# Two rows per block: summing the two partial results of an outer product before they are weighed, instead of weighing each

## The chip, the cores and the metric

The kernel runs on one core of a Trainium2 chip. A core has five engines that run their own queues in order: TensorE (PE, matrix multiplication into the accumulator memory PSUM), VectorE (DVE), ScalarE (ACT), GpSimd (POOL) and SyncE (SP), which here only issues transfers (DMA) between the main memory and the on-chip memory SBUF. PSUM has eight banks of 128 x 512 fp32 values. The metric is the time of one execution on the device in microseconds (us), given as the median of several runs.

## The reference

One layer of an encoder over a sequence of 2048 with 1024 features: an attention part and then a two-layer perceptron, each with a normalization ahead of it and a gate behind it. The change lies in the last line, in the second multiplication:

```
x = x + gt1 * (mixed @ w_o[l])
h = rmsnorm(x, g_norm2[l]) * (1.0 + sc2) + sh2
x = x + gt2 * (jnp.square(jax.nn.relu(h @ w1[l])) @ w2[l])
```

`w1` is 1024 x 4096 and `w2` is 4096 x 1024. The kernel holds everything transposed: features are rows, positions are columns. `gt2` is one factor per feature, so one per row.

## The kernel before, in words

**Seven products instead of eight, twice.** Both multiplications of the perceptron are done blockwise with the scheme that needs seven products of half-size blocks in place of eight (numbered 1 to 7 here); sums and differences of blocks are made ahead on VectorE. In the second multiplication, five of the seven products (`DOUBLE = (7, 2, 5, 3, 4)`, in this order) are cut once more in the same way. So each of these five is a stage of its own, made by the function `outer` and the class `Outer`, with seven inner products in the order `OUTER = (1, 5, 6, 3, 7, 2, 4)`. Here "stage 7" is the outer product 7, and "inner product 7" one of the seven in a stage. Products 1 and 6 (`PLAIN`) aren't cut again; product 1 runs ahead of stage 7, product 6 between stage 7 and stage 2.

**A step.** An inner product has eight steps (`HP`), a stage 56. A step does six matmuls: for each of two 128-row halves `n` of the result three, because every operand is held as a rounded high part and a remainder, and high x high, high x remainder and remainder x high are added up in PSUM (`mm3`). The high part is made by ScalarE (a cast), the remainder by VectorE (a subtraction); both go to one of eight operand buffers (pool `opp`, tile names `opr` for the moving operand, `ol` for two steps' worth of the fixed one). The planning loop at the end of the kernel prepares operands ahead of the step that multiplies as long as no more than eight of these buffers are taken. A step takes one and a half of them on average.

**Banks.** Inner products share accumulators (`HOME`): 1 and 2 add up in one pair of banks, 5 and 3 in a second, 6, 7 and 4 in a third, which starts as ScalarE's copy of the result of inner product 1. Four blocks of the result come out of this: block "12" is the second pair as it stands after inner product 3, plus the third pair as it stands after inner product 6. Block "22" is the second pair as it stands after inner product 5, plus the third pair as it stands after 7. Block "11" is the first pair after 2, block "21" the third pair after 4.

**Where a block goes.** A block of an outer product enters one block of rows of the output or two. Stages 2, 3 and 4 have one, stages 7 and 5 two ("two rows per block"). In `end`, called after the last step of an inner product for each half `n`, VectorE does for each target row tile `x`: x = (bank * gate) + x. This is `weigh`, one instruction on 128 x 512 values (SCALAR_TENSOR_TENSOR in the profile). The blocks "22" and "12" arrive in two parts, so their tiles are weighed into twice, once after each part: in stages 7 and 5 there are four weighings (two halves, two rows) after each of the inner products 5, 6, 3, 7, 2 and 4. After the last part of a block the tile is stored, by a transfer queued on SyncE two steps later (`later.add(2, ...)`): back to the scratch `scr_x`, or, where this was the row's last contribution, to the output.

**Rows.** The tiles `x` are loaded from `scr_x` by `load_x`, four per block in stages 7 and 5. Its step is counted from the start of the stage: block "22" at step 9, "12" at 11, "11" at 35, "21" at 43. Tiles come from two pools: `temp` (seven buffers; names in the profile begin with t, as `txo`) and `kept` (twelve buffers, names with c, as `cxo`). Four of the kept buffers hold the result of product 1 (`cs`) until stage 2 has used it.

**Order.** The queues of TensorE and SyncE follow the order of the program strictly. On VectorE and ScalarE instructions stand in the order in which the planning loop emits them: at each step first the preparation of operands ahead, then the jobs set for this step by `at` (among them the differences of operand tiles on 128 x 1024 values, `r<-r,r` in the profile, and the issue of loads), then the step's matmuls and what `end` adds, then the delayed stores.

In the profile all instructions have the line 42, that of a helper, so that tiles are told apart by name: `ps` and `ps_s` are accumulators (`ps_s` the pair that starts as a copy), `l` and `r` raw operands, `ol` and `opr` the prepared ones, `mod` holds the gates.

Of the kernel before, what the change touches and what calls it, by code (L numbers as in the profile page):

```python
# [13 lines left out]
ALU = mybir.AluOpType  # L14
# [65 lines left out]
def encoder_kernel(ctx, tc, xT, c, g1, g2, w_in, w_rest, gqk, bias, w_o, w1, w2, w_ada, b_ada, out):  # L80
    nc = tc.nc
    act, dve, pool, sp = nc.scalar, nc.vector, nc.gpsimd, nc.sync
# [161 lines left out]
    if True:  # L244
# [208 lines left out]
        def load_x(tb, q=None):  # L453
            xts[tb] = []
            for k in range(KT):
                xt = xp.tile([P, TB], F32, tag="xt", name=f"xt{tb}_{k}")
                (q or sp).dma_start(xt, xT[k * P : (k + 1) * P, tb * TB : (tb + 1) * TB])
                xts[tb].append(xt)
# [34 lines left out]
        act, dve, pool = (Ordered(tc, e) for e in (act, dve, pool))  # L493
# [7 lines left out]
        keep_busy(36, idle)  # L501
        act.activation(cg[:, 0:1], zero, AF.Sigmoid)
        load_x(3, osp)
        osp.dma_start(cb, c.partition_broadcast(P))
        osp.dma_start(bcol, b_ada)
# [64 lines left out]
        for k in range(KT):  # L570
# [18 lines left out]
            if k == KT - 3:  # L589
                load_raw(*loads.pop(0), osp)  # L590
                load_x(2, osp)
# [91 lines left out]
    if True:  # L683
# [68 lines left out]
        class Unit:  # L752


            def __init__(self, h, g, first, last):
                self.h, self.g, self.first, self.last = h, g, first, last
                self.nm = f"{self.ca}_{h}_{g}"
                self.ws = []
                self.wt = {}
# [19 lines left out]
            def values(self, j):  # L779
                if j == 0 and self.first:  # L780
                    pend["acc"] = ppo.tile([P, TB], F32, tag="acc", name=f"acc{self.nm}")
                self.acc = pend["acc"]
                wh, wl, cols, kb = self.wt.pop(j)
                end = self.last and j == len(self.blocks) - 1
                pe.matmul(self.acc[:, cols], self.v[:, kb, :], wh[:, cols], start=self.first and j == 0, stop=False)
                pe.matmul(self.acc[:, cols], self.v[:, kb, :], wl[:, cols], start=False, stop=end)
                if end:
                    soon.append(lambda: finish(self))
# [487 lines left out]
        for i in range(len(steps) + LAG):  # L1276
# [8 lines left out]
            done = list(soon)  # L1285
# [40 lines left out]
    PLAIN = (1, 6)  # L1326
    DOUBLE = (7, 2, 5, 3, 4)
    OUTER = (1, 5, 6, 3, 7, 2, 4)
    OUTER_NAME = {1: "11", 2: "12", 4: "22"}
    HOME = {1: 1, 2: 1, 5: 5, 3: 5, 6: 6, 7: 6, 4: 6}  # L1330
    HP = NP // 2
# [6 lines left out]
    if True:  # L1338
# [9 lines left out]
        def operand(src, nm, eng=None, dst=None):  # L1348

            o = opp.tile([P, 2, TB], F32R, tag="op", name=f"op{nm}") if dst is None else dst  # L1350
            split(o[:, 0, :], o[:, 1, :], src, eng)
            return o
# [8 lines left out]
        def column_sum(eng, out, a, b, op):  # L1361
            eng.tensor_tensor(out, a, b, op=op)
            return out
# [4 lines left out]
        def kept(nm):  # L1368
            return accp.tile([P, TB], F32, tag="c", name=f"c{nm}")

        def bank(nm, banks=pp):
            return banks.tile([P, TB], F32, tag="ps", name=f"ps{nm}")
# [3 lines left out]
        def at(n, job):  # L1376
            jobs.setdefault(n, []).append(job)
# [108 lines left out]
        class Step:  # L1486
            tiles = frees = 1

            def ready(self):
                return True  # L1490
# [7 lines left out]
        class First(Step):  # L1498
# [4 lines left out]
            def __init__(self, mb, j, i):  # L1503
                self.mb, self.j, self.i, self.nm = mb, j, i, f"{mb}_{j}_{i}"
                if mb and j == 0 and i in OUTER[:2]:
                    self.tiles = self.frees = 0

            def ready(self):
                return OUTER_NAME.get(self.i, self.i) in First.pair.get((self.mb, self.j), ())

            def prepare(self, home=None):
                if (home is None) != (self.tiles > 0):
                    return
                d, i = First.pair[self.mb, self.j], self.i
                self.w = operand(d[OUTER_NAME.get(i, i)], f"w{self.nm}", dst=home)

# [24 lines left out]
            def run(self):  # L1541
# [34 lines left out]
                if i == 4:  # L1576
                    c21 = self.hidden(kept(f"z{nm}"), 2, ps)

                    def end():
                        self.keep(4, column_sum(dve, kept(f"e{nm}"), c21, d["t2"], ALU.subtract))  # L1580
                        del First.pair[self.mb, self.j]

                    later.add(3, end)
# [98 lines left out]
        def weigh(x, a, n):  # L1682
            dve.scalar_tensor_tensor(x, a, mod[:, 5 * KT + n : 5 * KT + n + 1], x, op0=ALU.mult, op1=ALU.add)

        def rows_of(t, mb, n, odd):
            tb = 2 * mb + odd
            return t[n * P : (n + 1) * P, tb * TB : (tb + 1) * TB]
# [26 lines left out]
        def plain(mb, i):  # L1714

            f = len(steps)
            steps.extend(Second(mb, i, j) for j in range(NP))
            if i == 6:
                for n, step in enumerate((4, 5, 6, 12)):
                    update(mb, n, f + step, temp, False)  # L1720
            return f
# [48 lines left out]
        class Outer(Step):  # L1770
# [4 lines left out]
            def __init__(self, i, q, k):  # L1775
                self.i, self.q, self.pr, self.k = i, q, OUTER[q], k
                self.nm = f"{i}_{self.pr}_{k}"
# [43 lines left out]
            def end(self, n):  # L1821
                pr, ps = self.pr, Outer.banks[HOME[self.pr], n]
                if pr == 1:
                    Outer.banks[6, n] = bank(f"{self.nm}_s{n}", seeded)
                    act.copy(Outer.banks[6, n], ps)
                for b, done in {5: (("22", 0),), 6: (("12", 0),), 3: (("12", 1),), 7: (("22", 1),), 2: (("11", 1),), 4: (("21", 1),)}.get(pr, ()):
                    for x, mb, row, odd, last in Outer.outs[b, n]:
                        weigh(x, ps, row)
                        if done:
                            dst = rows_of(out, mb, row, odd) if last else scr_x[2 * mb + odd, row]  # L1830
                            later.add(2, lambda dst=dst, x=x: sp.dma_start(dst, x))

            def load_x(self, b):
                home = kept if self.i in (5, 7) and b in ("22", "11") else temp
                for n in range(2):
                    Outer.outs[b, n] = []
                    for r, odd in {2: ((0, 1),), 3: ((0, 0),), 4: ((1, 1),), 7: ((1, 1), (1, 0)), 5: ((0, 0), (1, 0))}[self.i]:
                        mb, row = 2 - int(b[1]), HK * r + 2 * (int(b[0]) - 1) + n
                        x = home(f"xo{self.i}_{b}_{n}{odd}")
                        sp.dma_start(x, scr_x[2 * mb + odd, row])  # L1840
                        Outer.outs[b, n].append((x, mb, row, odd, self.i in (2, 3, 4) or (self.i == 5 and r > 0)))
# [3 lines left out]
        def half(i, pr, g):  # L1845

            mb, a = {1: (1, 0), 5: (0, 0), 3: (0, 1), 2: (1, 1)}[pr]
            t = halves[pr, g] = hop[g].tile([P, 2, TB], F32, tag=f"h{pr}_{g}", name=f"r{i}_{pr}_{g}")
            sp.dma_start(t, scr_hid[mb, i, HP // 2 * a + g])

        def half_sum(i, pr, g):

            if pr == 5:
                column_sum(dve, halves[5, g], halves[5, g], halves[1, g], ALU.subtract)
                return
            x, y = {6: (3, 5), 7: (6, 1), 4: (2, 6)}[pr]
            t = hop[g].tile([P, 2, TB], F32, tag=f"h{pr}_{g}", name=f"r{i}_{pr}_{g}")
            column_sum(dve, t, halves[x, g], halves[y, g], ALU.subtract)
            halves[pr, g] = t

        def outer(i, plan):

            f = len(steps)
            steps.extend(Outer(i, q, k) for q in range(7) for k in range(HP))
            for g in range(HP // 2):
                for pr, (begin, gap) in plan["load"].items():
                    at(begin + gap * g, lambda pr=pr, g=g: half(i, pr, g))
                for pr, (begin, gap) in plan["sum"].items():
                    at(begin + gap * g, lambda pr=pr, g=g: half_sum(i, pr, g))
            for q in range(7):  # L1870
                at(f + HP * q - 12, steps[f + HP * q].load)
            for pr, b in ((5, "22"), (6, "12"), (2, "11"), (4, "21")):
                s = steps[f + HP * OUTER.index(pr)]
                at(f + HP * OUTER.index(pr) + (1 if b == "22" else -5), lambda s=s, b=b: s.load_x(b))
            return f

        class Mixed(Step):
# [45 lines left out]
        for mb in (1, 0):  # L1923
            begin = len(steps)
            steps += [First(mb, j, i) for j in range(NP) for i in OUTER]
            end = len(steps)
            for j in range(NP):
                f = steps[begin + 7 * j]
# [41 lines left out]
        f = plain(0, 1)  # L1970
# [4 lines left out]
        for i in DOUBLE:  # L1975
            f = outer(i, plan)
# [119 lines left out]
```

## Time and profile before

| | us |
|---|---|
| median of 3 runs | 2537.08 |
| lowest, highest | 2535.84, 2537.11 |
| the profiled execution | 2536.57 |
| its span, first to last instruction | 2534.8 |

The profile shows one execution. "Busy" is the time in which an engine had an instruction under way; VectorE's and ScalarE's instructions overlap their followers a little, so what an instruction costs its queue is read from start to start, not from its duration. Matmuls are pipelined: the duration of one is far longer than the distance to the next. In a list of instructions in order of time, equal neighbours are merged (x48), the first number is the start in us, and a bracket tells how long the engine was idle before and which engine's result ended it. SPq are transfers issued on SyncE's queue. The granted clock of TensorE was 0.998 over the span.

### The profile page before, as it was taken

What the parts mean: (1) busy time and instruction counts of PE and PEld (TensorE: products, weight loads), DVE (VectorE), ACT (ScalarE), POOL (GpSimd) and SP (SyncE); (2) the same over time, 40 slices, a digit from 0 to 9 for tenths busy, and PEclk for the clock granted to TensorE, in tenths of its full rate; (3) what the DMA queues carried; (4) which work ended last, traced back from release to release, by engine and by line L of the source; (5) the groups of instructions that cost most, each with busy time, mean ns of one, the idle gap of its engine ahead of it and who ended that gap; (6) DMA issues with size and microseconds to landing.
All of it is one profiled execution on the core that took longest, in us unless ns stands there. A gap on an engine that the chain in (4) does not pass through costs nothing.

```text
span 2534.8 us, 39551 instructions
## 1 busy us (share of the span) xinstructions
PE 2511.2 (99%) x12388; PEld 2097.2 (83%) x12388; DVE 2032.4 (80%) x3577; ACT 1523.8 (60%) x2917; POOL 773.9 (31%) x1160
## 2 busy tenths in 40 slices
PE   9999999999999999999999999999999999999999
PEld 8888888888878888788888888888888888888787
DVE  7656776887789988999868777779877759799998
ACT  6334424668866687666755555567555546576665
POOL 4330154776766677777620000000000000010000
PEclk9999999999999999999999999999999999999999
DMA  9879968779977788766777889996998996888882
GB/s 356 325 300 361 354 272 293 225 244 289 297 246 250 236 245 268 257 196 212 228 284 260 298 278 321 328 351 207 315 323 270 314 365 260 321 248 286 299 282 84
DMA packets 300755, 706.29 MB, mean 279 GB/s; under 512 B 32256, under 2 KB 91648, under 8 KB 288896
## 3 DMA queue, kind: packets, MB, share of 16 engines
q1 hardware_dynamic: 294640, 690.65, 79.5%
q0 software_dynamic: 4608, 8.39, 1.9%
q10 hardware_dynamic: 1296, 4.72, 0.5%
q8 instruction: 98, 1.61, 0.3%
q14 instruction: 113, 0.93, 0.1%
HBM read 476.61 MB, written 227.02 MB: 278 GB/s over the span
## 4 chain that ended last, share of the span: by engine, by line
PE 48%; DVE 7%; ACT 1%; DMA 1%; issue 1%; SPq 0%; POOL 0%; DVEq 0%; ACTq 0%; POOLq 0%
PE ps L42 25%; PE ps_s L42 14%; PE po L42 3%; PE acc L42 2%; PE wt L42 2%; DVE opr L42 2%; PE z L42 1%; DVE ol L42 1%; DVE r L42 1%; DVE h L42 1%; DVE txo L42 0%; PE cz L42 0%; ACT cy L42 0%; DVE cy L42 0%; ACT h L42 0%
## 5 line engine op out<-in xcount | busy, mean ns | idle before, releaser
L42 PE MATMUL ps<-h,opw 128*128 128x512 f32 x1512 | 358.6, 390 | 0.0
L42 ACT CAST wth<-wt 128x512 fp32r<-128x512 f32 (+3 forms) x544 | 257.1, 484 | 167.8 <-PE wt L42 157.1
L42 POOL TENSOR_TENSOR b<-p 128x512 f32<-128x512 f32 (+1 forms) x320 | 291.9, 912 | 167.1 <-DVE p L42 103.8
L42 DVE TENSOR_TENSOR wtl<-wt,wth 128x512 fp32r<-128x512 f32 (+3 forms) x544 | 291.0, 547 | 60.8 <-ACT wth L42 58.1
L42 PEld LDWEIGHTS ps<-h,opw 128*128 128x128 f32 x1512 | 283.9, 188 | 58.7
L42 PE MATMUL pt<-w,ht 128*128 128x512 f32 x1248 | 288.2, 391 | 0.0
L42 PE MATMUL ps_s<-h,opw 128*128 128x512 f32 x1152 | 277.5, 390 | 0.7 <-DVE cp L42 0.3
L42 PEld LDWEIGHTS pt<-w,ht 128*128 128x128 f32 x1248 | 233.1, 188 | 47.6
L42 DVE TENSOR_TENSOR_SCAN p<-z,p,zero 128x512 f32<-128x512 f32 x192 | 245.5, 1280 | 21.2 <-ACT z L42 16.4
L42 PEld LDWEIGHTS ps_s<-h,opw 128*128 128x128 f32 x1152 | 215.9, 188 | 46.7 <-DVE cp L42 0.9
L42 ACT CAST opr<-r 128x512 fp32r<-128x512 f32 x280 | 174.3, 623 | 129.1 <-PE ps L42 72.1
L42 PE MATMUL ps<-opr,ol 128*128 128x512 f32 x960 | 222.0, 390 | 0.4 <-DVE opr L42 0.3
L42 PE MATMUL acc<-wth,v 128*128 128x512 f32 (+3 forms) x544 | 220.9, 410 | 0.1
L42 PEld LDWEIGHTS ps<-opr,ol 128*128 128x128 f32 x960 | 179.9, 188 | 40.1 <-DVE opr L42 1.9
L42 ACT ACTIVATE z<-z 128x512 f32<-128x512 f32 (+1 forms) x320 | 166.5, 521 | 55.4 <-PE z L42 50.7
L42 DVE TENSOR_TENSOR opr<-r,opr 128x512 fp32r<-128x512 f32 x280 | 184.4, 681 | 10.8 <-ACT opr L42 10.0
L42 PE MATMUL z<-k,q 128*128 128x512 f32 (+3 forms) x640 | 185.8, 372 | 6.2 <-DVE p L42 5.5
L42 PE MATMUL acc<-wtl,v 128*128 128x512 f32 (+3 forms) x544 | 185.8, 348 | 0.1
L42 POOL DMA_DIRECT2D scr_x<-txu x12 | 10.5, 878 | 546.8 <-ACT txu L42 546.8
L42 PE MATMUL ps<-oph,opv 128*128 128x512 f32 x768 | 175.2, 390 | 0.3 <-DVE txo L42 0.2
L42 PE MATMUL wt<-ident,b 128*128 128x128 f32 x1088 | 171.2, 273 | 0.2 <-DVE p L42 0.2
L42 PEld LDWEIGHTS ps<-oph,opv 128*128 128x128 f32 x768 | 144.1, 188 | 30.9 <-DVE txo L42 0.6
(223 smaller groups left out, 5052.3 us busy)
## 6 DMA issues: line engine op xcount, KB each, us to landing
r<-scr_hid SPq DMA_DIRECT2D x80, 512.0 KB, 6.6
q<-scr_q SPq DMA_DIRECT2D x128, 256.0 KB, 5.3
w<-in_w_dram SPq DMA_DIRECT2D x64, 512.0 KB, 5.8
k<-scr_k SPq DMA_DIRECT2D x240, 128.0 KB, 4.1
v<-scr_v SPq DMA_DIRECT2D x120, 256.0 KB, 4.3
wa<-in_w_ada_dram SPq DMA_DIRECT2D x48, 512.0 KB, 6.2
ow<-scr_wo SPq DMA_DIRECT2D x24, 1024.0 KB, 6.7
l<-scr_t SPq DMA_DIRECT2D x20, 1024.0 KB, 7.7
```

The lines of the kernel that those rows point to most:

```text
L42: return lambda *x, **y: self.tc.keep_in_program_order(f(*x, **y))
```

## The change

In stages 5 and 7 the two parts of block "22" and of block "12" are no longer weighed one by one. After inner product 5 (block "22") and 6 (block "12") ScalarE copies the two banks to tiles of the kept pool. After inner product 7 (block "22") and 3 (block "12") VectorE adds the bank to this copy, and the sum is weighed into each of the two rows, once. The row tiles of "22" and "12" are therefore loaded later, five steps ahead of inner product 7 and of inner product 3 (steps 27 and 19). The row tiles of "22" and "21" come from the kept pool, those of "12" and "11" from the temporary one; before, "22" and "11" were kept. Blocks "11" and "21" are weighed as before, and the other three stages don't change.

```
+    TWICE = (5, 7)
...
                 for b, done in {5: (("22", 0),), 6: (("12", 0),), 3: (("12", 1),), 7: (("22", 1),), 2: (("11", 1),), 4: (("21", 1),)}.get(pr, ()):
+                    if self.i in TWICE and b[1] == "2":
+                        if not done:
+                            Outer.outs[b, n, "part"] = kept(f"q{self.nm}_{n}")
+                            act.copy(Outer.outs[b, n, "part"], ps)
+                            continue
+                        c = Outer.outs.pop((b, n, "part"))
+                        ps = column_sum(dve, c, ps, c, ALU.add)
                     for x, mb, row, odd, last in Outer.outs[b, n]:
                         weigh(x, ps, row)
...
             def load_x(self, b):
-                home = kept if self.i in (5, 7) and b in ("22", "11") else temp
+                home = kept if self.i in TWICE and b in ("22", "21") else temp
...
-            for pr, b in ((5, "22"), (6, "12"), (2, "11"), (4, "21")):
+            for pr, b in ((7 if i in TWICE else 5, "22"), (3 if i in TWICE else 6, "12"), (2, "11"), (4, "21")):
                 s = steps[f + HP * OUTER.index(pr)]
-                at(f + HP * OUTER.index(pr) + (1 if b == "22" else -5), lambda s=s, b=b: s.load_x(b))
+                at(f + HP * OUTER.index(pr) + (1 if pr == 5 else -5), lambda s=s, b=b: s.load_x(b))
```

## The prediction

> **What bounds the kernel now.** I read the page's first lines first, then the busy time by stretches of time, cut at the stages that the change touches.
>
> ```profile
> PE 2511.2 (99%) x12388; PEld 2097.2 (83%) x12388; DVE 2032.4 (80%) x3577; ACT 1523.8 (60%) x2917; POOL 773.9 (31%) x1160
> ```
> ```profile
> core 0: us, PE busy (x) PEld busy (x) DVE busy (x) ACT busy (x) POOL busy (x), PEclk, DMA share, GB/s
> 2101.60:2178.10 76.50, 76.50 (x338) 63.05 (x337) 74.77 (x114) 50.94 (x88) 0.00 (x0) 1.00 0.82 310
> 2298.20:2377.80 79.60, 78.43 (x337) 62.66 (x337) 79.60 (x120) 50.43 (x86) 0.00 (x0) 1.00 0.84 289
> ```
>
> TensorE bounds the whole. The two stretches are the outer stages of product 7 and product 5 of the second multiplication (stage 7, stage 5 below), the only ones that change. There VectorE is as full as TensorE: 74.77 of 76.50, and 79.60 of 79.60 us. Next, TensorE in order of time; a row starts where the accumulating bank changes, and 48 matmuls are one inner product.
>
> ```profile
> 2101.60 21.92 PE L42 MATMUL ps<-opr,ol 128*128 128x512 f32 x96
> ...
> 2156.00 11.38 PE L42 MATMUL ps<-opr,ol 128*128 128x512 f32 x48
> 2167.21 11.04 PE L42 MATMUL ps_s<-opr,ol 128*128 128x512 f32 x48
> 2178.09 1.52 PE L42 MATMUL ps<-oph,opv 128*128 128x512 f32 x6
> 2179.78 42.46 PE L42 MATMUL ps<-oph,opv 128*128 128x512 f32 x186 [0.17 <-DVE txo L42]
> ...
> 2298.24 21.92 PE L42 MATMUL ps<-opr,ol 128*128 128x512 f32 x96
> ...
> 2330.88 11.58 PE L42 MATMUL ps<-opr,ol 128*128 128x512 f32 x48
> 2342.30 5.83 PE L42 MATMUL ps_s<-opr,ol 128*128 128x512 f32 x25
> ...
> 2354.83 7.83 PE L42 MATMUL ps<-opr,ol 128*128 128x512 f32 x31
> ...
> 2366.94 11.04 PE L42 MATMUL ps_s<-opr,ol 128*128 128x512 f32 x48
> 2377.82 22.17 PE L42 MATMUL ps<-opr,ol 128*128 128x512 f32 x96
> ```
>
> An undisturbed inner product takes 10.88 us (2366.94 to 2377.82), a step (six matmuls) 1.36, a stage of seven 76.16. Stage 7 takes 2178.09 - 2101.60 = 76.49: 0.33 lost, all between 2156.00 and 2167.21, inner product 2. Stage 5 takes 79.58: 3.42 lost, of it 0.54 in inner product 3 (from 2330.88), 1.65 in 7 (from 2342.30), 1.23 in 2 (from 2354.83). So 3.75 us is nearly all that there is to win. VectorE in stage 7 says how the loss comes about; idle time before an instruction stands in brackets.
>
> ```profile
> 2132.37 0.69 DVE L42 TENSOR_TENSOR opr<-r,opr 128x512 fp32r<-128x512 f32 x1 [0.67 <-ACT opr L42]
> ...
> 2144.74 0.69 DVE L42 TENSOR_TENSOR opr<-r,opr 128x512 fp32r<-128x512 f32 x1
> 2145.34 2.72 DVE L42 SCALAR_TENSOR_TENSOR txo<-ps,mod,txo 128x512 f32<-128x512 f32 x4
> 2147.97 0.68 DVE L42 TENSOR_TENSOR opr<-r,opr 128x512 fp32r<-128x512 f32 x1
> ...
> 2157.47 2.72 DVE L42 SCALAR_TENSOR_TENSOR cxo<-ps_s,mod,cxo 128x512 f32<-128x512 f32 x4
> 2160.11 0.68 DVE L42 TENSOR_TENSOR opr<-r,opr 128x512 fp32r<-128x512 f32 x1
> ...
> 2161.31 1.22 DVE L42 TENSOR_TENSOR r<-r,r 128x1024 f32<-128x1024 f32 x1
> 2162.44 1.29 DVE L42 TENSOR_TENSOR opr<-r,opr 128x512 fp32r<-128x512 f32 x2
> ```
> ```profile
> 2143.95 0.62 ACT L42 CAST opr<-r 128x512 fp32r<-128x512 f32 x1 [0.22 <-PE ps L42]
> ```
> ```profile
> 2163.18 3.77 PEld L42 LDWEIGHTS ps<-opr,ol 128*128 128x128 f32 x17 [0.42 <-DVE opr L42]
> ```
>
> Four weighings at the end of an inner product occupy VectorE for 2.63 us (2145.34 to 2147.97), 0.66 each, and what stands behind them in its queue are remainders (opr, ol), which TensorE multiplies by. Up to 2144.74 VectorE keeps pace: at 2132.37 it stood idle for ScalarE's cast, and the cast waits for TensorE to give back an operand buffer. From 2145.34 on it never rests, is late by the end of inner product 7 (the weighings start at 2157.47, when inner product 2 has been running for 1.47), gets four more, and in inner product 2 the weight load at 2163.18 waits 0.42 for a remainder. In stage 5 the same queue was late before:
>
> ```profile
> 2320.86 2.71 DVE L42 SCALAR_TENSOR_TENSOR cxo<-ps,mod,cxo 128x512 f32<-128x512 f32 x4
> ...
> 2332.99 2.71 DVE L42 SCALAR_TENSOR_TENSOR txo<-ps_s,mod,txo 128x512 f32<-128x512 f32 x4
> ...
> 2345.12 2.71 DVE L42 SCALAR_TENSOR_TENSOR txo<-ps,mod,txo 128x512 f32<-128x512 f32 x4
> ...
> 2357.25 2.71 DVE L42 SCALAR_TENSOR_TENSOR cxo<-ps_s,mod,cxo 128x512 f32<-128x512 f32 x4
> ...
> 2362.22 1.27 DVE L42 TENSOR_TENSOR opr<-r,opr 128x512 fp32r<-128x512 f32 x2
> ```
>
> **The change part by part.** *Weighings removed.* Each stage loses four after inner product 5 and four after 6: 8 x 0.66 = 5.28 us of VectorE. *Sums added.* Two before the four weighings after 3, two before those after 7. These rows price them: a sum out of PSUM and its follower; two dependent sums; a weighing whose inputs all lie in SBUF.
>
> ```profile
> 1804.61 0.68 DVE L42 TENSOR_TENSOR cp<-ps,cp 128x512 f32<-128x512 f32 x1
> 1805.21 0.68 DVE L42 TENSOR_TENSOR opw<-w,opw 128x512 fp32r<-128x512 f32 x1
> ```
> ```profile
> 1813.08 0.68 DVE L42 TENSOR_TENSOR ca<-cp,cy 128x512 f32<-128x512 f32 x1
> 1813.80 0.69 DVE L42 TENSOR_TENSOR cb<-cp,ca 128x512 f32<-128x512 f32 x1
> ```
> ```profile
> 21.24 0.74 DVE L42 SCALAR_TENSOR_TENSOR ht<-xt,mod,ht 128x512 fp32r<-128x512 f32 x1
> 21.90 1.27 DVE L42 CUSTOM_DVE_ANT_0 wa<-wa,cs,bcol 128x1024 f32<-128x1024 f32 x1
> ```
>
> A sum holds the queue for 0.60 (1804.61 to 1805.21) if its follower doesn't need it, for 0.72 (1813.08 to 1813.80) if it does. The weighing behind each sum reads it, so I take s = 0.72. A weighing from SBUF takes 0.66 (21.24 to 21.90), as from PSUM: no change. The Trainium skill, "Perfetto Trace Analysis", section "Optimizing Scalar/DVE Operations", gives VectorE some 125 ns of access overhead on PSUM against 60 on SBUF; by it each of the 16 weighings would get about 0.065 us cheaper (an estimate from that page), 1.0 us off the result below. The two 0.66 steps of the rows don't bear it out, and I leave it out of the sum.
>
> *Stage 7.* The 5.28 us come off where VectorE had time: it can't run ahead, because its work waits for casts and those for buffers. What remains of the relief is that the remainder at 2144.74 can start when its cast (2143.95 + 0.62 = 2144.57) is done: 0.17 sooner. From there to the wait at 2163.18 VectorE has no gap, so every added us is a us for TensorE: 4 x 0.72 = 2.88. Loss afterwards 0.33 - 0.17 + 2.88 = 3.04 instead of 0.33: **+2.71**.
>
> *Stage 5.* Without the eight weighings the queue would reach the end of inner product 3 at 2345.12 - 5.28 = 2339.84, before TensorE (2330.88 + 10.88 = 2341.76): it has caught up, and stands as stage 7 does at that place. What follows has the same length in both: 12.13 us from the weighings after 3 to those after 7 (2145.34 to 2157.47; 2345.12 to 2357.25), 4.97 on to the remainders that TensorE waits for (2162.44; 2362.22). So it loses 3.04 too, instead of 3.42: **-0.38**.
>
> *ScalarE's copies,* four a stage:
>
> ```profile
> L42 ACT COPY cp<-ps 128x512 f32<-128x512 f32 x32 | 18.8, 588 | 32.2 <-PE ps L42 32.2
> L42 ACT CAST opr<-r 128x512 fp32r<-128x512 f32 x280 | 174.3, 623 | 129.1 <-PE ps L42 72.1 <-PE ps_s L42 47.5 <-DVE opr L42 8.1
> ```
>
> Two are 1.18 us after inner product 5 and again after 6, with a wait for the last matmuls; the casts behind them wait for those matmuls' buffers anyway, and have 129.1 / 280 = 0.46 us of slack each, so ScalarE is level again after three casts. The cover is the operand lead of eight buffers, 1.5 a step: five steps, 6.8 us. I cost them at nothing; without that cover it would be 1.18 for each pair. The banks copied are written again one inner product (10.88) later: no wait.
>
> *Loads of rows moved.* Sixteen a stage as before. "22" goes from step 9 to 27, "12" from 11 to 19, and they pass loads of operands on SyncE's queue.
>
> ```profile
> 2150.89 2.52 SPq L42 DMA_DIRECT2D l<-scr_s  x4
> ```
> ```profile
> DMA to landing us min/median/max: 4.9/6.4/11.4
> ```
>
> "12" has 12 steps, 16.3 us, before it is read. The tightest operand is that of inner product 4, whose issue (2150.89 to 2153.41) stands behind the stores of "12" and the loads of "11", which now take a fourth temporary that these stores set free. It moves by the two sums, 1.44, and with the longest landing of this tile, 11.4, arrives at 2166.3; cast and remainder (0.62 + 0.68) make 2167.6, and TensorE wants it at 2167.21 + 2.71 = 2169.92. Cost: nothing; beyond a landing of 13.7 us, one us for each us. The parts and "22" fill the twelve kept buffers of stage 7 together with the four sums of the plain stage; "21" takes the parts' buffers, which come free with the weighings that the stores ahead of it on SyncE's queue wait for anyway: nothing. No instruction is moved past another on GpSimd's queue. The 0.17 at 2179.78 stays: the wait in inner product 2 leaves VectorE just ahead of TensorE in both kernels.
>
> **Sum:** 2.71 - 0.38 = 2.33, in general 8s - 3.43. Profiled execution 2536.57 + 2.3 = 2538.9; it lies 0.51 below the median 2537.08, so 2539.4 as a median, slower by 0.09%.
>
> **Rivals.** *A, the relief carries over.* VectorE has 16 x 0.66 = 10.56 us of this work in a stage now, 4 x 0.72 + 8 x 0.66 = 8.16 then. If the 2.4 us counted as a total, both losses would vanish: -3.75, 2533.3. For it: 79.60 busy of 79.60 in stage 5. Against: the idle time at 2132.37 and the cast at 2143.95, which show that it can't work ahead of the second half. The same section of the Trainium skill's page would have work moved to ScalarE where VectorE is saturated; whether that holds where the work kept is bunched is what A decides.
>
> *B, the hand-over inside the sums is dearer (slower).* A weighing that waits for a sum out of PSUM is a pair that this trace doesn't have. The price is 8 us per us of s. It passes 0.2% (5.07 us) at s = 1.06; at 1.13, what the 128x1024 sums take (2161.31 to 2162.44), it gives 5.61 and 2542.7.
>
> *C, the operand of inner product 4 comes late* because of the moved loads: beyond the 13.7 us above. If it were 2.8 us later than that in one stage, 2542.2. Against: the longest landing of all is 11.4.
>
> **How the numbers follow.** 0.2% is about what a measurement of this kernel can tell from no change. My forecast: 0.64; s from 0.60 (independent) to 0.86 (0.74, the longest row, and 0.12 of hand-over) gives 1.37 to 3.45, its own range 2538.5 to 2540.5. A: 0.16, of it 0.06 for a gain of over 0.2%, more than the losses in these rows hold. B: 0.14. C and other delays: 0.06. Faster 0.06, same 0.64 + 0.10 = 0.74, slower 0.20. Cases of both signs are open, so the range runs from A's 2533.3 to B's 2542.7.
>
> **What would show it.** VectorE: four sums and eight weighings a stage with a copied part as input, sum to weighing 0.72. TensorE: stage 7 near 79.2 us, the lost time in inner products 7 and 2, its wait on a remainder; stage 5 near 79.2 with nothing lost in inner product 3. ScalarE: four copies a stage of 0.59. Wrong if stage 7 stays at 76.5 (A), if sum to weighing takes over 1 us (B), or if ScalarE waits for that operand's load (C).

## The result, and the profile after

| | before | after |
|---|---|---|
| median, lowest to highest of 19 runs each, us | 2536.73 (2535.25 to 2538.56) | 2540.56 (2538.40 to 2545.38) |
| the profiled execution, its span, us | 2536.57, 2534.8 | 2540.6, 2538.9 |
| stage 7: length less the undisturbed 76.16 | 0.33 | 4.19 |
| stage 5: the same | 3.42 | 4.49 |

The change makes the kernel slower, by a ratio of 1.0016 (95% interval 1.0010 to 1.0022). A second series with the same kernel, called "again" below, gave 2539.80 beside 2536.43, 1.0013 (1.0004 to 1.0022). The first line of the page, busy time by engine:

```profile
PE 2511.6 (99%) x12388; PEld 2096.6 (83%) x12388; DVE 2028.8 (80%) x3569; ACT 1527.8 (60%) x2925; POOL 773.9 (30%) x1160
```

VectorE is busy for 3.6 us less than before (2032.4), and the profiled execution takes 4 us more. TensorE of the kernel after, in order of time, stage 7 and then stage 5, the seven inner products in the order 1, 5, 6, 3, 7, 2, 4:

```profile
2101.10 21.92 PE L42 MATMUL ps<-opr,ol 128*128 128x512 f32 x96
...
2144.61 7.19 PE L42 MATMUL ps_s<-opr,ol 128*128 128x512 f32 x31
2151.96 4.15 PE L42 MATMUL ps_s<-opr,ol 128*128 128x512 f32 x17 [0.16 <-DVE opr L42]
2155.95 5.83 PE L42 MATMUL ps<-opr,ol 128*128 128x512 f32 x25
2163.22 7.50 PE L42 MATMUL ps<-opr,ol 128*128 128x512 f32 x23 [1.45 <-DVE opr L42]
2170.56 11.04 PE L42 MATMUL ps_s<-opr,ol 128*128 128x512 f32 x48
2181.44 4.82 PE L42 MATMUL ps<-oph,opv 128*128 128x512 f32 x19
...
2301.47 21.92 PE L42 MATMUL ps<-opr,ol 128*128 128x512 f32 x96
...
2344.99 7.19 PE L42 MATMUL ps_s<-opr,ol 128*128 128x512 f32 x31
...
2356.36 5.83 PE L42 MATMUL ps<-opr,ol 128*128 128x512 f32 x25
2363.61 2.16 PE L42 MATMUL ps<-opr,ol 128*128 128x512 f32 x6 [1.43 <-DVE opr L42]
...
2371.24 11.04 PE L42 MATMUL ps_s<-opr,ol 128*128 128x512 f32 x48
2382.12 4.24 PE L42 MATMUL ps<-opr,ol 128*128 128x512 f32 x18
```

From row to row, less 10.88 each: stage 7 loses 0.46 in inner product 7 (2144.61 to 2155.95) and 3.73 in 2 (2155.95 to 2170.56). Stage 5 loses 0.49 in 7 (2344.99 to 2356.36) and 4.00 in 2, and nothing ahead of that (2344.99 - 2301.47 is four times 10.88); inner product 3, which lost 0.54 before, is clean. Both waits are for a remainder from VectorE. VectorE of the same execution, around the end of inner product 3 and that of 7:

```profile
2129.15 0.69 DVE L42 TENSOR_TENSOR opr<-r,opr 128x512 fp32r<-128x512 f32 x1 [0.67 <-ACT opr L42]
...
2135.07 0.69 DVE L42 TENSOR_TENSOR opr<-r,opr 128x512 fp32r<-128x512 f32 x1 [1.15 <-ACT opr L42]
...
2140.03 0.69 DVE L42 TENSOR_TENSOR opr<-r,opr 128x512 fp32r<-128x512 f32 x1 [0.67 <-ACT opr L42]
...
2144.79 0.68 DVE L42 TENSOR_TENSOR cq<-ps,cq 128x512 f32<-128x512 f32 x1
2145.51 1.41 DVE L42 SCALAR_TENSOR_TENSOR txo<-cq,mod,txo 128x512 f32<-128x512 f32 x2
2146.84 0.68 DVE L42 TENSOR_TENSOR cq<-ps,cq 128x512 f32<-128x512 f32 x1
2147.55 1.41 DVE L42 SCALAR_TENSOR_TENSOR txo<-cq,mod,txo 128x512 f32<-128x512 f32 x2
2148.89 0.69 DVE L42 TENSOR_TENSOR opr<-r,opr 128x512 fp32r<-128x512 f32 x1
...
2158.39 0.68 DVE L42 TENSOR_TENSOR cq<-ps_s,cq 128x512 f32<-128x512 f32 x1
...
2162.48 0.69 DVE L42 TENSOR_TENSOR opr<-r,opr 128x512 fp32r<-128x512 f32 x1
```

Ahead of the end of inner product 3 VectorE stands idle again and again, for casts: the weighings taken away left holes there. Behind it the two sums and four weighings hold the queue for 4.10 us (2144.79 to 2148.89), where four weighings held it for 2.63 before, and again for 4.09 from 2158.39. A sum and its weighing are 0.72 apart (2144.79 to 2145.51).

One thing isn't in that list. TensorE of stage 7 by stretches: up to the long wait, the 4.4 us from its end, the rest:

```profile
core 0: us, PE busy (x) PEld busy (x) DVE busy (x) ACT busy (x) POOL busy (x), PEclk, DMA share, GB/s
2101.00:2163.00 62.00, 60.62 (x267) 49.53 (x265) 55.63 (x82) 43.48 (x76) 0.00 (x0) 1.00 0.73 282
2163.00:2167.40 4.40, 4.08 (x10) 2.99 (x11) 4.40 (x8) 0.62 (x1) 0.00 (x0) 0.61 0.93 307
2167.40:2181.40 14.00, 14.00 (x63) 11.58 (x62) 13.34 (x22) 8.84 (x15) 0.00 (x0) 1.00 1.02 397
```

For a few us behind its wait TensorE was granted 0.61 of its clock: ten matmuls in 4.40 us, where 63 took 14.00 afterwards (0.22 each). A mean of 0.61 over 4.40 us is half the clock for 3.4 us (0.39 x 4.40 x 2) and the whole for the rest. Stage 5 shows the same, 0.50 from 2365.36 to 2368.77. The execution profiled in the second series has the waits and not this drop:

```profile
2156.75 5.83 PE L42 MATMUL ps<-opr,ol 128*128 128x512 f32 x25
2163.97 2.02 PE L42 MATMUL ps<-opr,ol 128*128 128x512 f32 x6 [1.39 <-DVE opr L42]
2166.31 4.15 PE L42 MATMUL ps<-opr,ol 128*128 128x512 f32 x17 [0.32 <-DVE opr L42]
2170.30 4.92 PE L42 MATMUL ps_s<-opr,ol 128*128 128x512 f32 x21
```

Its stages lose 3.17 and 3.15. So the kernel's own loss is some 3.2 a stage, and the drop of the clock put 1.02 and 1.34 on top in the one execution.

### The profile page after: what moved, and what is told of

The parts are those of the page before. It is cut to its first block, busy times and chain, and to the rows that moved or that the text cites. A ratio compares the mean times of both kernels' runs of the same rounds, so it can differ in the third digit from the quotient of the medians.

```text
span 2538.9 us, 39556 instructions
## 1 busy us (share of the span) xinstructions
PE 2511.6 (99%) x12388; PEld 2096.6 (83%) x12388; DVE 2028.8 (80%) x3569; ACT 1527.8 (60%) x2925; POOL 773.9 (30%) x1160
## 4 chain that ended last, share of the span: by engine, by line
PE 52%; DVE 3%; DMA 2%; issue 1%; ACT 1%; SPq 0%; POOL 0%; DVEq 0%; ACTq 0%
PE ps L42 26%; PE ps_s L42 15%; PE po L42 3%; PE acc L42 2%; PE wt L42 2%; PE pso L42 2%; PE z L42 1%; DVE opr L42 1%; PE cz L42 0%; DMA ow<-scr_wo 0%; DMA scr_t<-twn 0%; DVE ol L42 0%; DMA scr_t<-wt 0%; DVE r L42 0%; DMA scr_hid<-cy 0%
```

## The experiments

Theory 1, of the prediction: VectorE is short in one place only, from the end of inner product 3 to the last wait in 2; what is added there is lost, and what is taken away ahead of it is not won, since VectorE can't work ahead. Rival A: the total of a stage's work decides. Rivals B and C: the pair of sum and weighing, or the moved loads. Theory 2, added after the first profile, puts the drop of the clock on top of theory 1. The table gives medians with the kernel before in the same series, and for each stage its length in one profiled execution less 76.16, with the inner products that lost (read off TensorE's rows as above).

| kernel | us (before) | ratio, 95% | stage 7 lost | stage 5 lost |
|---|---|---|---|---|
| no sums | 2533.43 (2536.72) | 0.9989 (0.9980 to 0.9997) | 0.32 | 0.29 |
| early loads | 2540.36 (2536.72) | 1.0016 (1.0007 to 1.0024) | 3.18 | 3.17 |
| spread weighings | 2537.57 (2536.72) | 1.0005 (0.9996 to 1.0014) | 2.17: 1.11 in 2, 1.06 in 4 | 2.22: 1.07 in 2, 1.15 in 4 |
| copies alone | 2536.61 (2536.72) | 0.9997 (0.9988 to 1.0006) | 0.37 | 3.47 |
| again | 2539.80 (2536.43) | 1.0013 (1.0004 to 1.0022) | 3.17: 0.49 in 7, 2.67 in 2 | 3.15: 0.49 in 7, 2.66 in 2 |
| two idle sums | 2538.27 (2536.43) | 1.0006 (0.9997 to 1.0015) | 1.63 in 2 | 3.43 |
| four idle sums | 2539.79 (2536.43) | 1.0012 (1.0003 to 1.0021) | 3.87 in 2 | 3.42 |
| GpSimd adds | 2549.59 (2536.43) | 1.0056 (1.0044 to 1.0069) | 8.38: 2.32 in 7, 6.06 in 2 | 9.05: 2.61 in 7, 6.44 in 2 |
| after, early differences | 2534.19 (2537.16) | 0.9991 (0.9982 to 1.0000) | 0.24 in 2 | 1.67: 1.18 in 7, 0.49 in 2 |
| before, early differences | 2538.33 (2537.16) | 1.0004 (0.9995 to 1.0013) | 0.83: 0.75 in 3 | 5.32: 0.43 in 6, 4.89 in 3 |
| GpSimd adds, idle | 2538.69 (2537.16) | 1.0009 (1.0000 to 1.0018) | 2.74: 1.76 in 6, 0.98 in 2 | 3.45 |
| after, differences far apart | 2535.61 (2536.92) | 0.9994 (0.9985 to 1.0003) | 0.24 in 2 | 1.69: 1.55 in 2 |

**Without the sums.**

```
-                        ps = column_sum(dve, c, ps, c, ALU.add)
+                        ps = c
```

> The changed kernel without the four sums a stage: the copied part alone is weighed into both rows (the part that arrives second is left out of blocks "22" and "12", so the output lacks it). Theory 1, VectorE's bunch: the four weighings after inner products 3 and 7 stay, the 2.9 us of sums before the wait go, so both stages lose about 0.2 us and the time is 3.4 us below the kernel before, near 2533.3. Theory 2, TensorE's clock on top of it (after a single wait of about 1.6 us it is granted half for 3.4 us): the same, and no stretch of half clock is left. Rival, the moved loads or ScalarE's copies: they are all still there, so the time stays near 2540.6.

TensorE of stage 5, from inner product 7 on:

```profile
2341.59 11.04 PE L42 MATMUL ps_s<-opr,ol 128*128 128x512 f32 x48
2352.47 11.34 PE L42 MATMUL ps<-opr,ol 128*128 128x512 f32 x48
2363.64 11.04 PE L42 MATMUL ps_s<-opr,ol 128*128 128x512 f32 x48
```

With the relief alone stage 5 keeps 0.29 of its 3.42 (2352.47 to 2363.64, less 10.88), stage 7 keeps its 0.32 as it was. So the relief is real in stage 5 and worth nothing in stage 7, and all that is lost on top comes with the sums.

**The loads where they were.**

```
-            for pr, b in ((7 if i in TWICE else 5, "22"), (3 if i in TWICE else 6, "12"), (2, "11"), (4, "21")):
+            for pr, b in ((5, "22"), (6, "12"), (2, "11"), (4, "21")):
```

> The changed kernel with the row tiles of "22" and "12" loaded where the kernel before loaded them (steps 9 and 11), the sums as they are. Theories 1 and 2: nothing hangs on these loads, 2540.6 within 1 us, stages 7 and 5 at 80.3 and 80.6 us, with the half clock in both or at least in some executions. Rival, the moved loads: back to about 2537.

3.18 and 3.17 against 3.17 and 3.15 with the loads moved, both without a drop of the clock: rival C is out.

**The copies alone,** put into the kernel before, into a tile that nobody reads:

```
+                if self.i in (5, 7) and pr in (5, 6):
+                    act.copy(np2.tile([P, TB], F32, tag="ndg", name=f"q{self.nm}_{n}", bufs=1), ps)
```

> The kernel before with ScalarE's four copies a stage added (after inner products 5 and 6, to a tile that nothing reads), and nothing else. Theories 1 and 2: covered by the operand lead, 2536.7 within 1 us. Rival, the copies hold back the casts: up to 4 us slower, and TensorE's waits in inner products 6 and 3.

0.04 a stage at most, and no difference in time that the runs can tell.

**The weighings of the sums put off** by two to five steps, one at a time, so that nothing stands bunched:

```
+                        def put(x=x, row=row, dst=dst, ps=ps):
+                            weigh(x, ps, row)
...
+                        if self.i in TWICE and b[1] == "2":
+                            later.add(2 + 2 * n + m, put)
+                        else:
+                            put()
```

> The changed kernel with the sums where they are, and the four weighings behind them put off by two, three, four and five steps, one a step (they read the sum in SBUF, so no bank waits for them). Same work, not in one bunch. Theory 1: what stands in front of the remainders at the end of inner products 3 and 7 falls from 4.1 to 1.4 us, the rest is spread over time that VectorE has later; stages 7 and 5 lose under 0.5 us each, 2533 to 2534. If instead the total of VectorE's work up to inner product 4 decides, each stage still loses about 3 us and the time is near 2539. Theory 2: no half clock.

The expectation failed: neither under 0.5 a stage nor the 3 of the total. The loss in inner product 7 is gone, but 2.2 a stage is left, and it comes later, in 2 and 4; the wait behind stage 7 grew too, from the 0.21 of the second series:

```profile
2162.47 4.58 PE L42 MATMUL ps<-opr,ol 128*128 128x512 f32 x17 [0.39 <-DVE opr L42]
2166.88 12.11 PE L42 MATMUL ps_s<-opr,ol 128*128 128x512 f32 x48
2178.82 1.52 PE L42 MATMUL ps<-oph,opv 128*128 128x512 f32 x6
2181.05 3.24 PE L42 MATMUL ps<-oph,opv 128*128 128x512 f32 x13 [0.70 <-DVE cxo L42]
```

Of the 1.0 saved in each stage about a half comes back behind it (that wait, and 0.68 in place of 0.24 in the stage behind stage 5). So the bunch as such costs little; most of the cost is how much VectorE has to do behind inner product 3: in inner product 7 twelve remainders of 0.60, two differences of 1.13 and the 4.1 for sums and weighings, 13.6 us, while TensorE needs 10.88; in 2 one difference less, 12.5. Put off, this work is late at another place. That sharpens theory 1: the short place reaches from the end of 3 to the end of the stage, and work that stays in this stretch is mostly lost wherever it stands.

**The change again, and the added cost by itself.** The kernel after, unchanged; and the kernel before with two or four dependent instructions of the size of a sum (a maximum, on an idle tile that VectorE clears once at step 9) behind inner product 7 of stage 7, on VectorE (shown with four):

```
+                if self.i == 7 and pr == 7 and n:
+                    for m in range(4):
+                        column_sum(dve, idle[0], idle[0], idle[0], ALU.max)
```

> The changed kernel once more, unaltered, for another profiled execution. Theory 1 alone (VectorE's queue sets the loss): the same loss in each execution, so stages 7 and 5 lose 4.2 and 4.5 us as in the first profile. Theory 2 (part of that was a half-clocked TensorE that comes with the long wait in some executions and not in others): each stage loses either 3.2 us without a half-clocked stretch or 4.2 to 4.5 with one, and the times scatter more widely than those of the kernel before.

> The kernel before with two dependent VectorE instructions of 0.72 us (on a tile that nothing reads) behind the four weighings after inner product 7 of stage 7 alone; all else as before. Theory 1: VectorE has no gap there, so stage 7 loses 0.33 + 1.44 = 1.8 us, the kernel 2538.2. If operands were ahead by enough to hide it: stage 7 stays at 0.3. Theory 2: the longest single wait is about 1 us, no half clock.

> The same with four such instructions. Theory 1: stage 7 loses 0.33 + 2.88 = 3.2 us, the kernel 2539.6. Theory 2: the wait before the first remainder is then about 2.4 us in one piece, longer than the 1.6 of the changed kernel; where it meets the half clock, 1 to 1.5 us more.

Two sums cost 1.30 (0.33 to 1.63), at 1.44 of VectorE's time: nine tenths goes through to TensorE. Four add 2.88 to the queue and cost 3.54, less than the 3.9 to 4.4 expected with the half clock and more than one for one. The clock dropped here too, in this row, behind a single wait, which can account for the excess:

```profile
2163.20 7.30 PE L42 MATMUL ps<-opr,ol 128*128 128x512 f32 x23 [1.79 <-DVE opr L42]
```

**GpSimd instead of VectorE.** VectorE makes the sums, ScalarE multiplies them by the gate (once where both rows have the same), GpSimd adds them to the rows (their stores two steps later, the load for inner product 4 four steps sooner):

```
+                                act.activation(y, ps, AF.Identity, scale=mod[:, 5 * KT + row : 5 * KT + row + 1])
...
+                            pool.tensor_tensor(x, x, y, op=ALU.add)
```

> The changed kernel with the sums on VectorE, but the weighing of the sum on other engines: ScalarE multiplies the sum by the gate, GpSimd adds it to each of the two rows (stored two steps later, the operand of inner product 4 loaded four steps sooner). Theory 1: VectorE has 1.4 us left after inner products 3 and 7 where the kernel before has 2.6, and nothing after 5 and 6; stages 7 and 5 lose nothing, 2533 or a little under. Rival, the copies, the stores or GpSimd's work count: stages 7 and 5 still lose 1 us or more.

Far slower: 2549.59 where 2533 was expected. VectorE, GpSimd and ScalarE behind inner product 3 of stage 7:

```profile
2148.42 0.77 DVE L42 TENSOR_TENSOR opr<-r,opr 128x512 fp32r<-128x512 f32 x1 [1.32 <-ACT opr L42]
2149.11 1.79 DVE L42 TENSOR_TENSOR ol<-l,ol 128x512 fp32r<-128x512 f32 x1
2150.82 2.31 DVE L42 TENSOR_TENSOR r<-r,r 128x1024 f32<-128x1024 f32 x1
2153.07 2.35 DVE L42 TENSOR_TENSOR opr<-r,opr 128x512 fp32r<-128x512 f32 x2
2155.34 0.68 DVE L42 TENSOR_TENSOR ol<-l,ol 128x512 fp32r<-128x512 f32 x1
```
```profile
2147.35 6.91 POOL L42 TENSOR_TENSOR txo<-txo,cq 128x512 f32<-128x512 f32 x4 [270.35 <-ACT cq L42]
```
```profile
2146.54 1.34 ACT L42 ACTIVATE cq<-cq,mod 128x512 f32<-128x512 f32 x2 [1.43 <-DVE cq L42]
```

Two costs take the place of the weighings. While GpSimd adds (2147.35 to 2154.26) VectorE's work from 2148.42 to 2155.34 takes 6.92 in place of 3.53 (four remainders of 0.60, one difference of 1.13): 3.4 lost. And ScalarE, waiting for the sums, holds back the casts behind, so that VectorE stands idle for 1.32. Together 4.7, against 2.64 saved: 2.1 worse for each of two blocks, on top of 3.17, makes 7.3 (an estimate from one block); measured are 8.38, and behind a wait of 2.49 in inner product 2 the clock drops again.

**GpSimd's additions alone:** four, on an idle tile, in the kernel before.

```
+                    for m in range(4):
+                        pool.tensor_tensor(idle[0], idle[0], idle[0], op=ALU.add)
```

> The kernel before, with four additions of 128 x 512 on GpSimd, on a tile that nobody else uses, issued behind inner product 7 of stage 7; no engine waits for them. In the version with GpSimd's additions VectorE's subtractions took 1.7 to 1.8 us in place of 0.68 while GpSimd was adding (6.9 us for four). Theory (the two engines hold each other up at SBUF): VectorE loses 6.9 x (1 - 0.68/1.75) = 4.2 us there, and stage 7 loses about 4.5 in place of 0.33; 2540.5 to 2542. Rival (it was ScalarE's queue, held back by its wait for the sums): VectorE's rows stay at 0.68, stage 7 at 0.33; 2536 to 2537.5.

They ran earlier than meant, since nothing on GpSimd's queue held them: as soon as the tile had been cleared.

```profile
2121.36 5.60 POOL L42 TENSOR_TENSOR idle<-idle 128x512 f32<-128x512 f32 x4 [241.82 <-DVE idle L42]
```
```profile
2121.65 1.53 DVE L42 TENSOR_TENSOR ol<-l,ol 128x512 fp32r<-128x512 f32 x1
2123.10 2.97 DVE L42 TENSOR_TENSOR opr<-r,opr 128x512 fp32r<-128x512 f32 x2
2125.99 1.52 DVE L42 TENSOR_TENSOR ol<-l,ol 128x512 fp32r<-128x512 f32 x1
2127.44 1.28 DVE L42 TENSOR_TENSOR opr<-r,opr 128x512 fp32r<-128x512 f32 x2
```

A remainder takes 1.45 from start to start while GpSimd adds (2121.65 to 2123.10) and 0.60 afterwards, and no engine waits for GpSimd here: this cost of the version above is shown by itself. The stage lost 2.74, less than the 4.5 expected for the fuller place, and the time, 2538.69, stayed below the 2540.5 to 2542 expected. The Trainium skill, "SBUF — State Buffer", section "SBUF: two separate sides", says that GpSimd and a VectorE instruction with two inputs in SBUF exclude each other for the whole instruction; the 1.45 in place of 0.60 fits that, though it doesn't tell turns from a lower speed of both.

**Work moved out of the short place.** If theory 1 holds, the holes ahead of the end of inner product 3 are worth something, once other work is put there. The differences for inner product 4 (`r<-r,r`, 1.13 each) were made at steps 28, 32, 36 and 40 of a stage; their sources are there earlier. In the kernel after, and for comparison in the kernel before:

```
-        plan["sum"] = {6: (f + 12, 2), 7: (f + 15, 2), 4: (f + 44, 4)}
+        plan["sum"] = {6: (f + 12, 2), 7: (f + 15, 2), 4: (f + 31, 4)}
...
-                plan["sum"] = {5: (e - 14, 3), 6: (e - 2, 4), 7: (e + 13, 4), 4: (e + 28, 4)}
+                plan["sum"] = {5: (e - 14, 3), 6: (e - 2, 4), 7: (e + 13, 4), 4: (e + 15, 4)}
```

> The changed kernel, with the four differences of 128 x 1024 for inner product 4 (1.13 us each) made at steps 15, 19, 23, 27 of stages 7 and 5 instead of 28, 32, 36, 40: three of them move from behind the sums of inner product 3 to ahead of them, where VectorE stood idle for ScalarE's casts. Theory (VectorE is short only between the end of inner product 3 and that of inner product 2, and idle ahead): 3.4 us go out of the short part, the bunch behind 7 and 2 is 4.1 + 12 x 0.60 = 11.3 us against 10.88, so a stage loses 0.2 to 0.8 instead of 3.17, no half clock; 2533.5 to 2535, faster than both kernels. Rival (a stage's total decides, or the hand-over from sum to weighing costs TensorE in some other way): stages still lose about 3; 2539 to 2540.5.

> The kernel before, with the same shift of four differences and nothing else. Theory: ahead of the end of inner product 3 VectorE has no idle time here in stage 5, so the 3.4 us only move the loss ahead: stage 5 loses 3 to 4 as before (3.43), stage 7 0 to 0.5; 2536 to 2537.5, no change. Rival (the place of the differences alone is worth the gain, without the sums): stage 5 loses under 1; 2533.5 to 2534.5.

The kernel after becomes the fastest of all that compute the whole: 2534.19, 3 us below before in the same series (0.9991, 0.9982 to 1.0000; the interval just reaches no change). Stage 7 loses 0.24 in place of 3.17. Stage 5 of that kernel, TensorE:

```profile
2342.44 5.83 PE L42 MATMUL ps_s<-opr,ol 128*128 128x512 f32 x25
2348.78 5.88 PE L42 MATMUL ps_s<-opr,ol 128*128 128x512 f32 x23 [0.51 <-DVE opr L42]
2354.50 11.54 PE L42 MATMUL ps<-opr,ol 128*128 128x512 f32 x48
2365.88 11.04 PE L42 MATMUL ps_s<-opr,ol 128*128 128x512 f32 x48
```

It still loses 1.67, more than expected, of it 1.18 in inner product 7 (2342.44 to 2354.50): here VectorE has no idle time left ahead of it. Eight differences stand there now, each with three remainders, 2.94 apart on VectorE (the first from 2318.59 to 2321.53), while TensorE takes 2.72 for the same two steps: the holes were smaller than what was put in, and the sums start at 2343.93, 1.5 after inner product 7 has begun. The same shift in the kernel before gains nothing, and the expectation (3 to 4 lost in stage 5, at most 0.5 in stage 7, 2536 to 2537.5) was missed: stage 5, where nothing was idle, loses 5.32 in place of 3.42, nearly all in inner product 3, behind a wait of 2.18 and with a drop of the clock in it; stage 7 loses 0.83. So neither half wins anything by itself, and both together do: the sums make room at one place, and the shift uses it.

**Differences far apart.** As the last, but in stage 5 at steps 20, 29, 38 and 47:

```
+                plan["sum"] = {5: (e - 14, 3), 6: (e - 2, 4), 7: (e + 13, 4), 4: (e + 20, 9)}
```

> As the version with the four differences moved to steps 15 to 27 in both stages, but in stage 5 they stand at steps 20, 29, 38 and 47. There VectorE had no idle time left with all four ahead of inner product 3's end, and the stage still lost 1.67 (1.18 in inner product 7, 0.49 in 2). Theory (VectorE's work up to the last wait, in inner product 2, is what counts once it has no idle time): the fourth difference, 1.13 us, goes behind that wait, where inner product 4 has 9.9 us of other work in 10.88; stage 5 loses 0.4 to 0.9, stage 7 0.24 as there, stage 3 at most 0.3 more; 2532.5 to 2534. Rival (only the place ahead of inner product 3's end helps): two of four stand behind it again, and stage 5 loses 2.2 to 2.7; 2534.5 to 2535.5.

The expectation failed: stage 5 loses 1.69 and the stage behind it 0.72 (0.25 before, nothing in the last version), and VectorE is idle once more ahead of the short place (0.39 before 2321.83). Together 2.4, as the rival had it for stage 5 alone; for stage 5 itself neither was right. The sums now start on time, at 2342.58, but one difference stands between them and those of inner product 7, at 2355.05: 12.47 us of work against 10.88, 1.6 too much, and 1.55 are lost in inner product 2. To move one difference behind the last wait doesn't pay for taking two out of the holes.

## Why the prediction was right

Predicted were 2539.4 and a slower kernel within 0.2%; measured are 2540.56 and 2539.80, 0.16% and 0.13%. The first lies just above the forecast's own range of 2538.5 to 2540.5, the second in it. By stage, where the clock held, +2.84 and -0.27 stand against the +2.71 and -0.38 of the sum.

*The relief, "stage 7: it can't run ahead".* Right, and shown: without the sums stage 7 keeps its 0.32, and with them VectorE stands idle for casts (1.15 at 2135.07) until 2140.03, 4.76 ahead of the first sum.

*"The loss afterwards 0.33 - 0.17 + 2.88 = 3.04".* Measured 3.17 where the clock held. The 0.17 was the term that was off. From the start of the stage to the end of the work ahead of the weighings or sums VectorE took 43.74 before (2101.60 to 2145.34) and 43.69 after (2101.10 to 2144.79): 0.05 sooner, not 0.17. The last cast didn't set it, as I had put it; VectorE has no gap from 2140.03 on, so its start there, released by an earlier cast, and the 4.76 of work behind it did.

*"It stands as stage 7 does".* Right: stage 5 loses 3.15, and by inner product the same as stage 7 (0.49 and 2.66; 0.49 and 2.67).

*s = 0.72.* Right (0.72 and 0.71), and rival B with it is out. The weighing out of SBUF takes 0.67 from start to start (2145.51 to 2148.89 holds four with one sum of 0.72 between: 2.66 / 4). What the Trainium skill, "Perfetto Trace Analysis", section "Optimizing Scalar/DVE Operations", states and the prediction set against the rows, VectorE's overhead smaller on SBUF than on PSUM, isn't borne out by these weighings: 0.67 against 0.66.

*Copies and loads at nothing.* Right: 0.04 a stage, and 3.18 against 3.17. The copies out of the second pair of banks, with durations in ns as lowest, median and highest (the other four, out of the third pair, have 587/587/589):

```profile
L42 ACT COPY cq<-ps x4: 587/588/589, 2122.4 to 2323.4; 128x512 f32<-128x512 f32 x4
```

*What the sum lacked* is the clock. It took the profiled execution 1.02 and 1.34 further. In the first series the kernel after scatters more widely, 2538.40 to 2545.38 beside 2535.25 to 2538.56; in the second it is the other way, 2539.07 to 2541.76 beside 2535.06 to 2542.89, so the scatter doesn't show it. Nor is every drop one of these two stages: five of the fourteen traces have one near 1047 us, far from the change. That it is the whole of what lies between the 2.6 us of the second profile (2.84 in stage 7, -0.27 in stage 5) and the 3.4 and 3.8 of the medians is argued, not shown; in how many executions it drops there was not measured.

*Rival A* was wrong for this kernel. That the time that it gave, 2533.3, is nearly what the kernel reaches once other work is moved into the holes (2534.19) is no proof of it: there the total of work in a stage is the same, and only its place differs.

## What to carry to other kernels

Ask of work that is taken off a full engine not how much it is but where in the queue it lay: ahead of the short place it leaves only holes, and what is added behind is lost nearly in full, though the engine's total falls. Before adding such a change, look for work whose inputs are ready early enough to be moved from the short place into the holes; here that turned some 3 us lost into some 3 us won, the latter with an interval that just reaches no change. And a long single wait of TensorE can cost more than itself, if the clock falls with it.

## What the runs showed of the hardware

- Behind single waits of 1.45 and 1.43 us TensorE was granted half its clock for 3.4 us in one execution; behind 1.39 to 1.45 in two others it was not. Behind 1.79, 2.18, 2.29 and 2.49 it was, behind 2.03 (GpSimd adds, stage 7, inner product 7) it was not. The Trainium skill, "TensorE: Matmul & The Clock Gate", section "Why this matters for your kernels", warns of gaps above some 3 us; here half of that was enough in some executions.
- More than the length of the wait, TensorE's idle time in a fixed stretch sorts these cases. The two drops of the first execution begin 201.39 us apart, 59 times their length of 3.413. The stretch of that length ahead of the first, and the drop (columns as in the result section):

```profile
2160.56:2163.97 3.41, 1.86 (x8) 1.01 (x7) 3.37 (x6) 1.43 (x3) 0.00 (x0) 1.00 0.75 292
2163.97:2167.38 3.41, 3.41 (x9) 2.64 (x10) 3.41 (x6) 0.62 (x1) 0.00 (x0) 0.50 0.91 284
```

TensorE was idle for 3.41 - 1.86 = 1.55 us, and for 1.52 ahead of the second drop (2361.95 to 2365.36). In the stretches of the same grid that hold the waits of the second series it was idle for 1.48 and 1.36 (from 2161.14 and 2362.53), in those of the early loads for 1.45 and 1.47 (from 2161.30 and 2362.68), and the clock held. Over all fourteen traces, without the first 60 and the last 20 us and counted where the clock was full, the eleven stretches ahead of a drop have 1.52 or more, and none with 1.48 or less has a drop behind it; two with more have none either, 1.54 (before, early differences, from 1043.46) and 1.81 (the wait of 2.03, from 2153.06). So about 1.5 us of 3.41 is where it began here, and the rule isn't complete.

- While GpSimd added 128 x 512 tiles, VectorE's subtractions took 1.45 us from start to start (on an idle tile) and up to 1.71 (on the row tiles) in place of 0.60.
- A sum out of PSUM and a weighing that reads it are 0.72 apart, like two dependent sums in SBUF.
